# Merge stage of a decoder trunk: raw tiles of their own for the second attention's results, and two blocks' gates loaded ahead of them

## The chip, the cores and the metric

The kernel runs on one core of one Trainium2 chip. The time is the device time of that core in microseconds, from the first instruction to the last; the kernel before takes 1337.81 us (median of 3 runs, 1337.39 to 1337.92). Engines are named as in the profile: PE multiplies matrices (PEld is its weight load), DVE and POOL are the two elementwise engines, ACT evaluates functions and copies, SP issues DMAs in the order in which they stand in its queue. Each engine executes its own list in order; engines wait for each other through semaphores.

## What is computed

One layer of a decoder trunk on 1024 tokens of width 1024: a norm, two attentions side by side, a gated merge of their results, a residual, and a gated MLP with a short convolution. The part that matters here is the merge:

```python
def reference(x, ...):
    xn = rmsnorm(x, norm_mix_w[l])
    proj = xn @ w_in[l]
    da_q, da_k, da_v, sw_q, sw_k, sw_v, g_da, g_sw = split_cols(proj)
    ...
    y_da = diff_attention(da_q, da_k, da_v, lam, lam_init, subln_w[l])
    y_sw = sliding_window_attention(sw_q, sw_k, sw_v, sinks[l])
    merged = jax.nn.sigmoid(g_da) * (y_da @ w_br_da[l]) + jax.nn.sigmoid(g_sw) * (y_sw @ w_br_sw[l])
    x = x + merged @ w_mix_out[l]
    ...
```

Both results `y_da` and `y_sw` are 1024 tokens by 512 channels; everything is float32.

## The kernel before

Tensors lie transposed, channels on the 128 partitions and the 1024 tokens (T) along the row; a tile of [P, T] is 128 x 1024 floats, 512 KB. A product in float32 is made of three products of rounded parts: an operand is split into a high part (`h`, a cast on ACT) and a low part (`l`, the difference, on DVE), and PE adds `wh*xh`, `wh*xl` and `wl*xh` (lines 212 to 214). Half of T, 512 columns, is one matmul.

The two attentions write their results to `yd` in DRAM, 8 tiles: 0 to 3 from the differential attention, 4 to 7 from the sliding-window attention (the second attention), whose last piece is stored by ACT's queue at the very end of that stage. The gates' raw products lie in `gd`, 16 tiles.

`rest` is the stage after the attentions, the merge. It has three steps.

1. Loop over c = 0..7: load `yd[c]` into a raw tile `yr`, and split it into `yh[c]` (ACT, line 836) and `yl[c]` (DVE, line 837). The raw tiles come from a pool `yrp` of 4, so that tile 4 takes the place of tile 0 when that has been split, and so on. Between them the last four half blocks of the gates' projection are computed on PE (`back_half`, matmuls `g<-xh,wh`, lines 212 to 214).
2. For each output block m = 0..7, `first(m)`: take the block's weights (`next_w`: load, `wh` on ACT line 177, `wl` on DVE line 179); load the block's two gates `gr` (line 796), multiply them by the norm factor on POOL (line 797), take the sigmoid on ACT (line 804); multiply the first attention's four tiles with the weights into the PSUM tile `sc`; and multiply gate 0 by `sc` on DVE (line 808). For m = 0 the products with `yl` stand last (line 203).
3. `second(m)`: the same product for the second attention's four tiles, in two halves of T into PSUM tiles `g` from a pool of 2; DVE multiplies gate 1 by each half (line 816), adds the two branches (line 821), and the sum is split again (lines 822, 823).

The order is `first(0), first(1), second(0), second(1)`, then `first(m), second(m)` for m = 2..7. The gates have 4 tiles in all, so the first two blocks' gates fill them. A scheduler orders each engine's list from the program's order and priorities; `tc.high_priority(200)` in step 1 lets the loads of `yd` go ahead of what is written before them. A DMA in SP's queue that has to wait for a tile holds all that stand behind it. After step 3, `mix` multiplies the merged tiles with the next weights.

## Time and profile before

| what | value |
|---|---|
| median of 3 runs | 1337.81 us |
| the profiled execution: its own time | 1339.47 us |
| the profiled execution: its span, first to last instruction | 1337.7 us |
| mean granted TensorE clock | 0.997 |
| last store of the second attention's results issued | 499.86 us |
| merge stage, first high part of `yd` to first matmul of the mix | 502.1 to 606.5 us |
| loads of the second four `yd` tiles: issue to landing, shortest, median, longest | 3.2, 5.8, 7.5 us |
| all 16 gate loads: issue to landing, shortest, median, longest | 3.1, 4.0, 8.7 us |

The times of the rows are counted from the span's start. In a view of the timeline a row is: start, duration, engine, line, operation, result<-operands, shapes, how many in a row, and in brackets the idle time of the engine before it with what ended it. Ends of matmuls are modelled: a matmul of 512 columns is shown with 0.39 us, while the next starts 0.227 us after it.

### The profile page before, as it was taken

How to read it: one execution, taken by the hardware profiler on the slowest of the kernel's cores; microseconds unless marked ns; L12 is line 12 of the kernel's file. 1: busy time of each engine (PE TensorE's matmuls, PEld its weight loads, DVE VectorE, ACT ScalarE, POOL GpSimd, SP SyncE). 2: the span in 40 equal slices, each digit the busy share in tenths (PEclk: the TensorE clock that was granted, in tenths of full speed). 3: DMA queues.
4: the chain of work that ended last, by engine and by line, in shares of the span. 5: the costliest groups of instructions: out<-in, count | busy, mean ns of one | idle time of the engine just before them, and what ended most of it. 6: DMA issues, size and time to landing. Idle time of an engine off the chain costs nothing.

```text
span 1337.7 us, 17292 instructions
## 1 busy us (share of the span) xinstructions
PE 1319.4 (99%) x6264; PEld 1096.8 (82%) x6264; DVE 1075.5 (80%) x1607; ACT 624.4 (47%) x1023; POOL 483.1 (36%) x363
## 2 busy tenths in 40 slices
PE   7999999999999999999999999999999999999997
PEld 6888888888888777888888888888888888888887
DVE  8847775289889877765678999999999997879975
ACT  8432232176667766433445443344444444323553
POOL 0336543000102113521436556555565520214532
PEclk9999999999999999999999999999999999999998
DMA  7423443866553335434432222222222229672263
GB/s 259 145 107 142 158 158 142 251 179 174 157 128 125 104 112 212 149 117 132 136 111 84 90 93 82 80 78 95 79 96 75 75 84 332 214 279 67 95 173 126
DMA packets 63621, 183.69 MB, mean 137 GB/s; under 512 B 6960, under 2 KB 15280, under 8 KB 63536
## 3 DMA queue, kind: packets, MB, share of 16 engines
q1 hardware_dynamic: 51504, 164.13, 37.5%
q10 hardware_dynamic: 11456, 17.41, 3.6%
q0 software_dynamic: 576, 1.05, 0.5%
q8 instruction: 49, 0.80, 0.3%
q14 instruction: 36, 0.29, 0.1%
HBM read 130.66 MB, written 50.86 MB: 136 GB/s over the span
## 4 chain that ended last, share of the span: by engine, by line
PE 93%; DVE 3%; POOL 1%; issue 1%; DMA 1%; ACT 1%; POOLq 0%; SPq 0%; ACTq 0%; DVEq 0%
PE t L924 13%; PE t L923 13%; PE t L925 13%; PE g L212 4%; PE g L213 4%; PE g L214 4%; PE sc L213 3%; PE sc L214 3%; PE sc L212 3%; PE t L917 3%; PE sc L639 3%; PE y L1167 2%; PE d L1167 2%; PE d L924 2%; PE d L923 2%; PE d L925 2%
## 5 line engine op out<-in xcount | busy, mean ns | idle before, releaser
L1097 ACT ACTIVATE c<-us,vecs 128x512 f32<-128x512 f32 x80 | 61.3, 781 | 134.0 <-POOL us L1091 130.0
L1099 DVE SCALAR_TENSOR_TENSOR c<-us,vecs,c 128x512 f32<-128x512 f32 x160 | 110.5, 748 | 8.6 <-ACT c L1097 8.6
L1091 POOL TENSOR_TENSOR us<-us,rstd 128x1024 f32<-128x1024 f32 x38 | 99.7, 2643 | 4.5 <-DVE us L472 2.4
L129 DVE TENSOR_TENSOR sl<-sf,sh 128x1024 fp32r<-128x1024 f32 x62 | 86.6, 1399 | 11.5 <-ACT sh L128 11.5
L128 ACT CAST sh<-sf 128x1024 fp32r<-128x1024 f32 x62 | 63.4, 1049 | 59.8 <-PE t L924 43.5
L129 DVE TENSOR_TENSOR wl<-raw,wh 128x1024 fp32r<-128x1024 f32 (+1 forms) x35 | 76.6, 2190 | 3.7 <-ACT wh L128 3.6
L177 ACT CAST wh<-raw 128x1024 fp32r<-128x1024 f32 (+2 forms) x46 | 46.2, 1005 | 67.8 <-PE sc L213 30.4
L104 POOL TENSOR_TENSOR sf<-rv 128x512 f32<-128x512 f32 x30 | 41.3, 1377 | 100.7 <-DVE sl L129 57.8
L212 PE MATMUL g<-xh,wh 128*128 128x512 f32 x176 | 70.7, 402 | 0.1
L214 PE MATMUL g<-xh,wl 128*128 128x512 f32 x176 | 70.4, 400 | 0.0
L213 PE MATMUL g<-xl,wh 128*128 128x512 f32 x176 | 70.2, 399 | 0.0
L179 DVE TENSOR_TENSOR wl<-raw,wh 128x1024 fp32r<-128x1024 f32 (+2 forms) x46 | 53.8, 1169 | 17.5 <-PE t L609 11.0
L109 POOL TENSOR_TENSOR sf<-raw,rv 128x512 f32<-128x512 f32 x30 | 40.8, 1359 | 66.0 <-DVE sl L129 66.0
L643 DVE CUSTOM_DVE_ANT_0 L<-sc,bias 128x128 f32<-128x128 f32 (+7 forms) x64 | 47.8, 752 | 17.0 <-PE sc L639 13.9
L622 POOL MEMSET aT<- 128x128 f32 x32 | 6.2, 205 | 151.6 <-PE t L668 97.9
L797 POOL TENSOR_TENSOR gr<-gr,rstd 128x1024 f32<-128x1024 f32 x16 | 41.0, 2566 | 52.9 <-DMA gr<-gd 43.5
L644 ACT ACTIVATE L<-L,sm 128x128 f32<-128x128 f32 (+7 forms) x64 | 49.6, 779 | 20.0 <-DVE sm L643 13.5
L129 DVE TENSOR_TENSOR wl<-rv,wh 128x512 fp32r<-128x512 f32 x30 | 49.8, 1661 | 3.5 <-ACT wh L128 3.5
L1101 ACT ACTIVATE c<-c 128x512 f32<-128x512 f32 x40 | 24.0, 600 | 60.7 <-DVE c L1099 60.7
L639 PE MATMUL sc<-u,u 128*128 128x512 f32 (+2 forms) x192 | 49.7, 358 | 0.0
L878 POOL TENSOR_TENSOR rstd<-rstd,t 128x512 f32<-128x512 f32 x14 | 21.7, 1558 | 76.1 <-ACT t L877 76.1
L212 PE MATMUL sc<-mh,wh 128*128 128x512 f32 x126 | 49.0, 389 | 0.0
(529 smaller groups left out, 4423.6 us busy)
## 6 DMA issues: line engine op xcount, KB each, us to landing
u<-qd SPq DMA_DIRECT2D x72, 256.0 KB, 6.2
raw<-in_w_in SPq DMA_DIRECT2D x25, 512.0 KB, 4.1
raw<-in_w_up SPq DMA_DIRECT2D x23, 512.0 KB, 3.5
hr<-hd SPq DMA_DIRECT2D x46, 256.0 KB, 5.7
hd<-c SPq DMA_DIRECT2D x22, 512.0 KB, 2.6
rv<-in_w_up SPq DMA_DIRECT2D x21, 512.0 KB, 3.5
raw<-in_w_down SPq DMA_DIRECT2D x19, 512.0 KB, 4.1
gr<-gd SPq DMA_DIRECT2D x16, 512.0 KB, 4.0
```

The source lines that it names most:

```text
L128: i = nc.scalar.copy(hi, src)
L129: j = nc.vector.tensor_tensor(lo, src, hi.bitcast(F32), ALU.subtract)
L212: nc.tensor.matmul(ps, wh[:, kc + o, :], ah, start=first and n == 0, stop=False)
L213: nc.tensor.matmul(ps, wh[:, kc + o, :], al, start=False, stop=False)
L214: nc.tensor.matmul(ps, wl[:, kc + o, :], ah, start=False, stop=last and n == len(kcs) - 1)
L639: nc.tensor.matmul(sc[:, lo + n0:lo + n1], qs, k[c][part][:, n0:n1], start=part == 0, stop=part == 1)
L923: nc.tensor.matmul(ps, ah[:, k, :], bh, start=first and n == 0, stop=False, skip_group_check=skip)
L924: nc.tensor.matmul(ps, ah[:, k, :], bl, start=False, stop=False, skip_group_check=skip)
L925: i = nc.tensor.matmul(ps, al[:, k, :], bh, start=False, stop=last and n == len(ks) - 1, skip_group_check=skip)
L1091: (nc.vector if j == 0 else nc.gpsimd).tensor_tensor(u[:, 2:], u[:, 2:], self.rstd, ALU.mult)
L1097: nc.scalar.activation(c, u[:, o + 2:o + 2 + H2], AF.Identity, bias=self.vecs[:, C_CB + m:C_CB + m + 1], scale=col(m, 2))
L1099: nc.vector.scalar_tensor_tensor(c, u[:, o + k:o + k + H2], col(m, k), c, ALU.mult, ALU.add)
```

## The change

The second attention's four raw tiles get a pool of their own, `ysp`, so that they no longer wait for the first four to be split. Ahead of them, at priority 300, the four gates of the first two blocks are loaded; `first` takes these and loads the gates itself only for the later blocks.

```diff
                 bp = bctx.enter_context(tc.tile_pool(name="bp", bufs=2, reuse_waits="tile"))
+                ysp = bctx.enter_context(tc.tile_pool(name="ysp", bufs=4, reuse_waits="tile"))
                 parts = []
+                gates = {}
                 for c in range(8):
+                    if c == 4:
+                        with tc.high_priority(300):
+                            for m in range(2):
+                                gates[m] = [self.tl(bp, [P, T], "gr", bufs=4) for _ in range(2)]
+                                for br, g in enumerate(gates[m]):
+                                    nc.sync.dma_start(g, self.gd[8 * br + m])
                     with tc.high_priority(200):
-                        r = self.tl(yrp, [P, T], "yr")
+                        r = self.tl(ysp if c > 3 else yrp, [P, T], "yr")
                         nc.sync.dma_start(r, self.yd[c])
...
                     for br in range(2):
-                        g = self.tl(bp, [P, T], "gr", bufs=4)
-                        nc.sync.dma_start(g, self.gd[8 * br + m])
+                        if m in gates:
+                            g = gates[m][br]
+                        else:
+                            g = self.tl(bp, [P, T], "gr", bufs=4)
+                            nc.sync.dma_start(g, self.gd[8 * br + m])
                         i = nc.gpsimd.tensor_tensor(g, g, self.rstd, ALU.mult)
```

No instruction is added or left out; the lists have the same length. From line 779 on the new file's line numbers are higher (783 becomes 791, 797 becomes 808, 804 becomes 815, 808 becomes 819, 816 becomes 827, 836 and 837 become 847 and 848).

SP's queue at the turn from attention to merge, before. The names are those of the tiles above; `gr_5078` and `gr_5082` are block 0's gates, `gr_5118` and `gr_5122` block 1's; the semaphores DMAHW tell of the landing of earlier DMAs, which share eight of them.

```order
L796 DMA gr_5078<-gd 128x1024 [waits DMAHW1_49,PE_49,Pool_49]
L796 DMA gr_5082<-gd 128x1024 [waits DMAHW2_49,PE_49,Pool_49]
L783 DMA yr_5044<-yd 128x1024 [waits DMAHW6_49,DMAHW5_49,DMAHW7_49,DMAHW3_49,DVE_49]
L783 DMA yr_5050<-yd 128x1024 [waits DMAHW4_49,DVE_49]
L783 DMA yr_5056<-yd 128x1024 [waits DMAHW7_49,DMAHW5_49,DVE_49]
L783 DMA yr_5062<-yd 128x1024 [waits DVE_49]
L796 DMA gr_5118<-gd 128x1024 [waits DMAHW0_49,Pool_49]
L796 DMA gr_5122<-gd 128x1024 [waits DMAHW1_49]
```

The same place of SP's queue in the changed kernel (block 0's gates are `gr_5047` and `gr_5048`, block 1's `gr_5051` and `gr_5052`):

```order
L788 DMA gr_5047<-gd 128x1024 [waits DMAHW1_49,PE_49,Pool_49]
L788 DMA gr_5048<-gd 128x1024 [waits DMAHW2_49,PE_49,Pool_49]
L788 DMA gr_5051<-gd 128x1024 [waits DMAHW3_49,Pool_49]
L788 DMA gr_5052<-gd 128x1024 [waits DMAHW4_49]
L791 DMA yr_5055<-yd 128x1024 [waits DMAHW6_49,DMAHW7_49,DMAHW5_49,Pool_49]
L791 DMA yr_5061<-yd 128x1024 [waits DMAHW7_49]
L791 DMA yr_5067<-yd 128x1024 [waits DMAHW0_49]
L791 DMA yr_5073<-yd 128x1024 [waits DMAHW1_49]
```

Block 1's two gates have moved ahead of the four loads of `yd`, and these no longer wait for DVE. The waits for Pool in both are for POOL's work in the attention stage.

DVE's list at the start of the merge, before:

```order
L837 TENSOR_TENSOR yl_4933<-yr_4930,yh_4932 128x1024
L837 TENSOR_TENSOR yl_4967<-yr_4964,yh_4966 128x1024
L837 TENSOR_TENSOR yl_5007<-yr_5004,yh_5006 128x1024
L837 TENSOR_TENSOR yl_5041<-yr_5038,yh_5040 128x1024
L179 TENSOR_TENSOR wl_5076<-raw_5072,wh_5074 128x1024
L837 TENSOR_TENSOR yl_5047<-yr_5044,yh_5046 128x1024
L837 TENSOR_TENSOR yl_5053<-yr_5050,yh_5052 128x1024
L837 TENSOR_TENSOR yl_5059<-yr_5056,yh_5058 128x1024
L837 TENSOR_TENSOR yl_5065<-yr_5062,yh_5064 128x1024
L808 TENSOR_TENSOR gr_5078<-gr_5078,sc_5086 128x1024
L808 TENSOR_TENSOR gr_5118<-gr_5118,sc_5126 128x1024
L816 TENSOR_TENSOR gr_5082<-gr_5082,g_5152 128x512
```

and in the changed kernel:

```order
L848 TENSOR_TENSOR yl_4936<-yr_4933,yh_4935 128x1024
L848 TENSOR_TENSOR yl_4970<-yr_4967,yh_4969 128x1024
L848 TENSOR_TENSOR yl_5010<-yr_5007,yh_5009 128x1024
L848 TENSOR_TENSOR yl_5044<-yr_5041,yh_5043 128x1024
L179 TENSOR_TENSOR wl_5087<-raw_5083,wh_5085 128x1024
L819 TENSOR_TENSOR gr_5047<-gr_5047,sc_5093 128x1024
L848 TENSOR_TENSOR yl_5058<-yr_5055,yh_5057 128x1024
L848 TENSOR_TENSOR yl_5064<-yr_5061,yh_5063 128x1024
L848 TENSOR_TENSOR yl_5070<-yr_5067,yh_5069 128x1024
L819 TENSOR_TENSOR gr_5051<-gr_5051,sc_5129 128x1024
L848 TENSOR_TENSOR yl_5076<-yr_5073,yh_5075 128x1024
L827 TENSOR_TENSOR gr_5048<-gr_5048,g_5155 128x512
```

The two products of a gate with `sc` have moved in between the second attention's low parts: block 0's ahead of all four, block 1's ahead of the last. On ACT the sigmoids of block 0's second gate and of block 1's first gate have moved ahead of the casts `yh` of the second attention's tiles. PE's list differs in one place: in `second(0)` the last two matmuls of the first half (those with the last `yl` and with `wl`) have moved behind the first two of the second half. POOL's list is the same: the first two blocks' four gates, one after the other, then the later blocks' gates.

## The prediction

> **What bounds the kernel now.** First the page's busy shares and its chain by engine: PE works 99% of the span and holds 93% of the chain. What the change is worth is therefore the time that PE stands still at the start of the merge, and no more.

> ```profile
> PE 1319.4 (99%) x6264; PEld 1096.8 (82%) x6264; DVE 1075.5 (80%) x1607; ACT 624.4 (47%) x1023; POOL 483.1 (36%) x363
> PE 93%; DVE 3%; POOL 1%; issue 1%; DMA 1%; ACT 1%; POOLq 0%; SPq 0%; ACTq 0%; DVEq 0%
> ```

> Then the busy time by stretch (a row begins with the stretch, its length and PE's busy time; clock, DMA share and GB/s end it): PE is idle between 517.2 and 525.1 alone, and not at all in the rest of the merge.

> ```profile
> 500.00:517.20 17.20, 17.20 (x77) 14.24 (x76) 11.55 (x8) 11.43 (x12) 4.79 (x2) 1.00 0.70 264
> 517.20:525.10 7.90, 6.02 (x26) 4.33 (x25) 4.30 (x5) 4.79 (x5) 5.64 (x2) 1.00 0.50 202
> 525.10:606.00 80.90, 80.90 (x357) 67.00 (x358) 55.17 (x47) 29.04 (x29) 30.55 (x12) 1.00 0.38 130
> ```

> PE's timeline shows the two places.

> ```profile
> 519.30 0.39 PE L212 MATMUL g<-yh,wh 128*128 128x512 f32 x1
> 519.83 0.50 PE L213 MATMUL g<-yl,wh 128*128 128x512 f32 x1
> 520.17 0.40 PE L214 MATMUL g<-yh,wl 128*128 128x512 f32 x1
> 522.91 0.39 PE L214 MATMUL g<-yh,wl 128*128 128x512 f32 x1
> 525.03 0.50 PE L212 MATMUL g<-yh,wh 128*128 128x512 f32 x1 [1.73 <-DVE gr L816]
> 525.37 0.40 PE L213 MATMUL g<-yl,wh 128*128 128x512 f32 x1
> ```

> Matmuls otherwise start 0.227 us apart (511.82 to 512.27 below is two steps). From 519.30 to 519.83 is 0.53, so 0.30 is lost, and 0.11 more, since the one after a wait follows after 0.34. From 522.91 to 525.03 is 2.12: 1.89 lost, and again 0.11. Together 0.41 + 2.00 = 2.41 us. The chain of waits says what the longer one hangs on:

> ```profile
> 509.99 0.32 SPq L783
> 510.41 8.26 DMA gr<-gd
> 518.74 3.30 POOL gr L797
> 522.06 1.07 ACT gr L804
> 523.16 1.22 DVE gr L808
> 524.38 0.61 DVE gr L816
> ```

> Block 1's first gate is issued behind the last load of `yd`, lands 8.26 us later, and goes through POOL, ACT and DVE; only then comes line 816, which frees the PSUM tile that PE needs for `second(1)`.

> **What is taken away.** Block 1's gates are issued right behind block 0's, whose loads were issued by 494.98 + 3.57 = 498.55 and landed 4.0 and 5.6 us after their issue; over all gate loads the longest took 8.7.

> ```profile
> 494.98 3.57 SPq L796 DMA_DIRECT2D gr<-gd  x2
> DMA to landing us min/median/max: 4.0/4.8/5.6
> DMA to landing us min/median/max: 3.1/4.0/8.7
> ```

> So they land between 502.6 and about 508 instead of 518.7, and line 816 of block 0 needs no gate of block 1 any more. The second attention's loads then wait only for stores, the last issued at 499.86:

> ```profile
> 499.86 0.39 ACTq L560 DMA_DIRECT2D yd<-ys  x1
> DMA to landing us min/median/max: 1.8/3.2/8.7
> DMA to landing us min/median/max: 3.2/5.8/7.5
> ```

> With the longest landing of a store (8.7, second row) and of these loads (7.5, third row) they are there by 516.1, which is early enough for all that follows. Their cost is nothing: SP has no other work there. Gain if nothing else moved: 2.41 us.

> **What is added.** No instruction. But POOL's multiplies of block 1's gates move too: from 518.7, where DVE was mostly reading PSUM, to right behind block 0's, that is onto DVE's run of low parts.

> ```profile
> 500.69 4.79 POOL L797 TENSOR_TENSOR gr<-gr,rstd 128x1024 f32<-128x1024 f32 x2 [7.44 <-DMA gr<-gd]
> 503.23 6.74 DVE L837 TENSOR_TENSOR yl<-yr,yh 128x1024 fp32r<-128x1024 f32 x4 [3.56 <-ACT yh L836]
> 506.48 3.49 DVE L837 TENSOR_TENSOR yl<-yr,yh 128x1024 fp32r<-128x1024 f32 x3
> 509.89 1.21 DVE L179 TENSOR_TENSOR wl<-raw,wh 128x1024 fp32r<-128x1024 f32 x1
> 510.01 1.98 PE L203 MATMUL sc<-yl,wh 128*128 128x512 f32 x8
> 511.82 0.39 PE L212 MATMUL sc<-yh,wh 128*128 128x512 f32 x1
> 512.27 0.39 PE L214 MATMUL sc<-yh,wl 128*128 128x512 f32 x1
> ```

> The first low part starts at 503.23 and does not end before POOL does (500.69 + 4.79 = 505.48); three more follow 1.14 us apart ((3.49 - 1.21)/2), the fourth ends at 509.97, block 1's `wl` at 511.10. PE's eight products with `yl` come at 510.01, each pair just in time, and the first with `wl` at 512.27. The cover is thin: 1.17 us for `wl`, 1.4 for the last `yl` (509.97 against the last pair, at 510.01 + 6 x 0.227 = 511.37).

> [...]

> ```profile
> 698.19 2.27 POOL L109 TENSOR_TENSOR sf<-raw,rv 128x512 f32<-128x512 f32 x1
> 700.43 2.27 POOL L108 TENSOR_TENSOR sf<-sf,raw 128x512 f32<-128x512 f32 x1
> 702.77 1.30 POOL L110 TENSOR_TENSOR sf<-raw,sf 128x512 f32<-128x512 f32 x1
> 695.89 1.22 DVE L837 TENSOR_TENSOR T_2l<-t,T_2h 128x1024 fp32r<-128x1024 f32 x1
> 697.02 2.29 DVE L837 TENSOR_TENSOR T_3l<-xw,T_3h 128x1024 fp32r<-128x1024 f32 x1
> 699.24 2.31 DVE L129 TENSOR_TENSOR wl<-raw,wh 128x1024 fp32r<-128x1024 f32 x1
> ```

> They take turns, one instruction each: DVE's ends at 699.31 and 701.55 are 2.24 apart instead of 1.14, POOL's rows last 2.27 where one alone lasts 1.30. A POOL instruction let in between thus delays DVE by 1.10, its own 1.30 less 0.20. A gate multiply alone lasts 2.42:

> ```profile
> L797 POOL TENSOR_TENSOR gr<-gr,rstd x16: 2388/2418/3292, 500.7 to 584.7; 128x1024 f32<-128x1024 f32 x16
> ```

> so each costs 2.22. The third and fourth gates have landed while DVE is still in its run (505.48 to 511.10), so I let both in: 4.44 us. The fourth `yl` ends at 514.41, `wl` at 515.54. PE does the last pair with `yl` at 514.46 (0.05 for the semaphore), starts `first(1)` at about 515.0 and its first product with `wl` at 515.59 instead of 512.27: 3.32 later, with 0.11 for the restart 3.4. Whether POOL's two go in ahead of the second and third `yl` or later does not matter: the end of `wl` counts both. Bounds: none let in, 0; one, 2.22 less, which is 1.2; both, 3.4.

> The moved line 808 on DVE (819 now) takes one operand from PSUM and is not delayed: at 523.16 above it lasted 1.22 while POOL was at work (518.74 and 5.64 us on, by the second row of the stretches). That of block 1 stands ahead of the last `yl` and waits for the end of `first(1)`: `second(0)` starts at 517.26 + 3.4 = 520.7 (517.26 is 511.82 and 24 steps), line 819 runs 1.2 us from about 520.9, the last `yl` ends at 523.3, and PE, whose list has two other matmuls ahead of it now, needs it at 520.7 + 11 x 0.227 = 523.2. About 0.2 with the restart. Line 816 then frees its PSUM tile at about 524.8, well ahead of `second(1)` at 526.3: the longer stall is gone.

> **The sum.** 3.4 - 2.41 + 0.2 = +1.2 us. After 525 every wait is counted from PE's, DVE's or POOL's own progress and PE has no idle time to fill or to save, so the shift stays to the end. The profiled execution takes 1339.47 (its span 1337.7), 1.7 over the median of the runs shown; the same shift gives 1340.7 there, and on the median 1337.81 a forecast of **1339.0**. With small waits more or less, the forecast's own range is 1338.0 to 1339.8.

> **Rivals.** [...] *Only one gets in* because the fourth gate lands after DVE's run is over: 1.2 - 2.22 = -1.0, so 1336.8; the landing would have to be later than the longest of the 16.

> *The clock drops.* My sum makes PE wait from about 511.1 to 513.3 for the third `yl` (the turns end it at 513.27), and some 0.4 us more for the fourth. In the tail the granted clock (third number from the end) is 1.00, then 0.50, after a stretch with nothing but 12 narrow matmuls:

> ```profile
> 1327.70:1329.70 2.00, 1.47 (x12) 1.30 (x11) 0.77 (x4) 1.58 (x4) 0.08 (x1) 1.00 0.84 296
> 1329.80:1337.70 7.90, 1.12 (x4) 0.72 (x4) 1.88 (x3) 0.37 (x1) 1.78 (x2) 0.50 0.44 152
> ```

> That is 2 us of little work; the wait of 1.73 us above left it at 1.00. So the point from which this decides lies near 2 us in one piece. At half clock a matmul takes 0.454. No row shows how long it lasts in work: between nothing and the 7.9 us of the tail, a loss of 0 to 4.0; halfway, 2.0: 1339.0 + 2.0 = 1341.0, slower. Against it: PE is busy before, between and after the two waits, and the tail is one case. [...]

> **Chances.** Forecast 0.62; port no matter 0.13; one gets in 0.10; clock drops 0.15. Range for 8 in 10: from the first rival, 1335.4, to 1340.5, which leaves out most of the clock's case. A measurement of this kernel tells a change from none at about 0.2%, 2.7 us. Faster by that (under 1335.1) would need more than all the idle time of the stage: 0.04. Slower by that (over 1340.5) is the clock's case, most of it: 0.13. Within: 0.83.

> **What would show it.** POOL's four multiplies in a row from 500.7 with the later ones lasting 3.3 instead of 2.4; low parts of 3.3 us on DVE; `wl` ending at 515.5; a wait of about 2.2 us on PE among the products of line 203, released by DVE's `yl`; no wait at `second(1)`; the first matmul of the mix some 1.2 us later. Wrong if the four low parts end by 510 with POOL busy beside them, if block 1's gates land after 510, or if the clock's row in 510 to 520 is under 1.00.

## The result, and the profile after

| | before | after |
|---|---|---|
| median of 11 runs each | 1337.81 us | 1340.88 us |
| lowest and highest run | 1336.05, 1339.88 | 1338.69, 1342.42 |
| profiled execution: own time, span | 1339.47, 1337.7 | 1341.0, 1339.2 |

The ratio is 1.0021, with a 95% interval of 1.0012 to 1.0029: 1.6 to 3.9 us slower. The forecast was 1339.0 and the range ended at 1340.5. The direction was right, the size was not: the time is that of a rival, *the clock drops*, at 1341.0.

First the two engines that were to take turns, POOL and then DVE, on the timeline of the kernel after (start, duration, engine, line, what, how many; in brackets the idle time ahead and what ended it):

```profile
500.53 11.46 POOL L808 TENSOR_TENSOR gr<-gr,rstd 128x1024 f32<-128x1024 f32 x4 [7.60 <-DMA gr<-gd]
```

```profile
502.91 11.30 DVE L848 TENSOR_TENSOR yl<-yr,yh 128x1024 fp32r<-128x1024 f32 x4 [3.57 <-ACT yh L847]
514.14 1.21 DVE L179 TENSOR_TENSOR wl<-raw,wh 128x1024 fp32r<-128x1024 f32 x1
```

POOL's four multiplies run in a row, and the four low parts take 11.30 us instead of 6.74. The single instructions end in turn: DVE's first at 506.39, POOL's third at 508.67, DVE's second at 509.75, POOL's fourth at 511.99, DVE's third at 513.08. Block 1's `wl` ends at 515.35 (515.5 forecast). PE's timeline shows what that does to block 0's products with `yl` (line 203), and one thing more:

```profile
509.69 1.07 PE L203 MATMUL sc<-yl,wh 128*128 128x512 f32 x4
513.13 0.73 PE L203 MATMUL sc<-yl,wh 128*128 128x512 f32 x2 [2.37 <-DVE yl L848]
514.27 1.22 PE L203 MATMUL sc<-yl,wh 128*128 128x512 f32 x2 [0.40 <-DVE yl L848]
515.28 0.63 PE L212 MATMUL sc<-yh,wh 128*128 128x512 f32 x1
515.71 0.63 PE L213 MATMUL sc<-yl,wh 128*128 128x512 f32 x1
516.14 0.63 PE L214 MATMUL sc<-yh,wl 128*128 128x512 f32 x1
516.56 0.63 PE L212 MATMUL sc<-yh,wh 128*128 128x512 f32 x1
516.99 0.49 PE L213 MATMUL sc<-yl,wh 128*128 128x512 f32 x1
517.32 0.39 PE L214 MATMUL sc<-yh,wl 128*128 128x512 f32 x1
```

The wait of 2.37 us, ended by DVE's third `yl`, is the one forecast at about 2.2. Behind it the matmuls start 0.427 apart (515.28, 515.71, 516.14) instead of 0.227. The view by stretch gives the clock granted there; a row is the stretch, its length, the busy time of PE, PEld, DVE, ACT and POOL, and then the granted clock, the DMA share and GB/s:

```profile
506.95:510.36 3.41, 3.41 (x16) 2.81 (x15) 3.41 (x2) 3.38 (x5) 3.41 (x2) 1.00 0.63 200
510.36:513.77 3.41, 1.04 (x4) 0.30 (x2) 3.41 (x2) 3.41 (x5) 1.63 (x1) 1.00 0.89 363
513.77:517.19 3.42, 3.02 (x8) 2.37 (x8) 3.17 (x4) 1.84 (x2) 0.00 (x0) 0.50 0.16 44
517.19:520.60 3.41, 3.41 (x17) 2.78 (x16) 3.03 (x3) 0.00 (x0) 0.00 (x0) 1.00 0.76 233
...
521.60:529.50 7.90, 7.90 (x36) 6.45 (x36) 5.19 (x6) 2.22 (x3) 0.00 (x0) 1.00 0.23 66
```

For 3.41 us the clock is at half, right behind a stretch of the same length in which PE was busy for 1.04 us only. The last row holds `second(0)`, which starts at 521.66, and the start of `second(1)` at 527.12, the two places at which the kernel before lost its 2.41 us: PE is busy for all of it, so both old waits are gone.

The first matmul of the mix shows the sum, before and then after:

```profile
595.88 0.39 PE L212 MATMUL sc<-mh,wh 128*128 128x512 f32 x1
```

```profile
597.84 0.39 PE L212 MATMUL sc<-mh,wh 128*128 128x512 f32 x1
```

Below, *the stage* is the time from the first product with `yh` (506.38 before, 506.06 after) to this matmul: 89.50 us before, 91.77 after. (The 606.5 us in the table ahead of the prediction is the time of a later matmul of the mix; the first stands at 595.88.) It is freer of chance than the whole time, which also holds what differs between runs ahead of the stage and in the tail.

### The profile page after: what moved, and what is told of

Its sections match the earlier page's. It is cut to its first block, busy times and chain, and to the rows that moved or that the text cites. A ratio compares the mean times of both kernels' runs of the same rounds, so it can differ in the third digit from the quotient of the medians.

```text
span 1339.2 us, 17291 instructions
## 1 busy us (share of the span) xinstructions
PE 1320.1 (99%) x6264; PEld 1097.4 (82%) x6264; DVE 1082.9 (81%) x1607; ACT 623.5 (47%) x1023; POOL 484.0 (36%) x363
## 4 chain that ended last, share of the span: by engine, by line
PE 94%; DVE 3%; POOL 1%; issue 1%; ACT 1%; DMA 0%; POOLq 0%; SPq 0%; ACTq 0%; DVEq 0%
PE t L936 13%; PE t L935 13%; PE t L934 13%; PE g L212 4%; PE g L213 4%; PE g L214 4%; PE sc L212 3%; PE sc L213 3%; PE sc L214 3%; PE t L928 3%; PE sc L639 3%; PE y L1178 2%; PE d L1178 2%; PE d L935 2%; PE d L934 2%; PE d L936 2%
## 5 line engine op out<-in xcount | busy, mean ns | idle before, releaser
L129 DVE TENSOR_TENSOR sl<-sf,sh 128x1024 fp32r<-128x1024 f32 x62 | 87.4, 1412 | 11.5 <-ACT sh L128 11.5
L129 DVE TENSOR_TENSOR wl<-raw,wh 128x1024 fp32r<-128x1024 f32 (+1 forms) x35 | 76.7, 2191 | 3.7 <-ACT wh L128 3.6
L212 PE MATMUL g<-xh,wh 128*128 128x512 f32 x176 | 70.6, 401 | 0.1
L214 PE MATMUL g<-xh,wl 128*128 128x512 f32 x176 | 70.4, 400 | 0.0
L213 PE MATMUL g<-xl,wh 128*128 128x512 f32 x176 | 70.3, 399 | 0.0
L179 DVE TENSOR_TENSOR wl<-raw,wh 128x1024 fp32r<-128x1024 f32 (+2 forms) x46 | 53.8, 1169 | 18.3 <-PE t L609 11.0
L109 POOL TENSOR_TENSOR sf<-raw,rv 128x512 f32<-128x512 f32 x30 | 40.7, 1356 | 65.6 <-DVE sl L129 65.6
L808 POOL TENSOR_TENSOR gr<-gr,rstd 128x1024 f32<-128x1024 f32 x16 | 41.4, 2596 | 54.6 <-DMA gr<-gd 45.3
L129 DVE TENSOR_TENSOR wl<-rv,wh 128x512 fp32r<-128x512 f32 x30 | 49.3, 1642 | 3.5 <-ACT wh L128 3.5
L212 PE MATMUL sc<-mh,wh 128*128 128x512 f32 x126 | 49.0, 389 | 0.0
```

The lines of the kernel that those rows point to most:

```text
L129: j = nc.vector.tensor_tensor(lo, src, hi.bitcast(F32), ALU.subtract)
L212: nc.tensor.matmul(ps, wh[:, kc + o, :], ah, start=first and n == 0, stop=False)
L213: nc.tensor.matmul(ps, wh[:, kc + o, :], al, start=False, stop=False)
L214: nc.tensor.matmul(ps, wl[:, kc + o, :], ah, start=False, stop=last and n == len(kcs) - 1)
```

## The experiments

In the kernels' expectations, "the whole change" is the kernel after. Table of all profiled executions, each time from the trace: the stage; from the first product with `yh` to the start of `second(0)`, and from there to `second(1)`; whether a stretch of half clock stands in the merge; the median time (number of runs); and the ratio to the kernel before on the same chip.

| kernel | stage | to `second(0)` | to `second(1)` | half clock | median us | ratio, 95% interval |
|---|---|---|---|---|---|---|
| before | 89.50 | 10.88 | 7.77 | no | 1337.81 (11) | |
| b1, before again | 89.07 | 10.88 | 7.31 | no | 1338.47 (1) | |
| b2, before again | 88.62 | 10.88 | 6.88 | no | 1337.44 (1) | |
| after | 91.77 | 15.60 | 5.46 | yes | 1340.88 (11) | 1.0021 [1.0012, 1.0029] |
| a1, after again | 91.28 | 15.10 | 5.46 | yes | 1341.15 (1) | |
| a2, after, a third time | 92.17 | 16.01 | 5.44 | yes | 1340.62 (12) | 1.0022 [1.0013, 1.0031] |
| e1, tiles only | 88.03 | (other order) | | no | 1337.41 (11) | 0.9996 [0.9987, 1.0004] |
| e2, gates only | 91.57 | 15.36 | 5.49 | yes | 1341.12 (11) | 1.0021 [1.0012, 1.0030] |
| e3, multiplies held | 88.34 | 10.88 | 6.74 | no | 1337.90 (11) | 1.0000 [0.9991, 1.0008] |
| e5, held, and ACT's order | 88.19 | 10.88 | 6.59 | no | 1337.52 (11) | 0.9999 [0.9990, 1.0008] |
| e4, wait filled, 9 | 90.07 | 13.91 | 5.44 | no | 1340.31 (11) | 1.0015 [1.0006, 1.0023] |
| e6, wait filled, 9 on two tiles | 89.95 | 13.79 | 5.44 | no | 1340.60 (11) | 1.0019 [1.0010, 1.0027] |
| e7, wait filled, 4 | 89.98 | 13.82 | 5.44 | no | 1340.80 (12) | 1.0022 [1.0013, 1.0030] |
| e8, wait filled, 2 | 90.01 | 13.85 | 5.44 | no | 1341.19 (8) | 1.0025 [1.0014, 1.0036] |

Medians of the kernel before, run beside them, were 1337.91 (e1 to e4), 1337.49 (b1, b2, a1, e5), 1337.82 (a2, e6, e7) and 1337.91 (e8).

### e1: the tiles alone

```diff
-                    if c == 4:
+                    if False:
```

> The second four results keep tiles of their own (ysp); the gates of blocks 0 and 1 are loaded where the kernel before loaded them, so that those of block 1 are issued behind the last yr load. Theory (DVE and POOL take turns; the wait that this makes on PE halves the clock for one 3.41 us stretch): block 1's gates land after the first four yl are done, POOL has only block 0's two multiplies beside them, and block 0's low products start as before: no wait of 2.4 us before them, no 0.50 clock row in the merge. From the first yh product to the first mix matmul 87.1 to 89.5 us (before 89.50, whole change 91.77), the time 1335.4 to 1338 us. Rival (the new tiles are what delays the merge, through the loads' order): a wait of 2 us or more stays before the products of L203 and the stage takes 91 us or more, as in the whole change.

```profile
511.18 11.11 POOL L808 TENSOR_TENSOR gr<-gr,rstd 128x1024 f32<-128x1024 f32 x4 [18.55 <-DMA gr<-gd]
```

```profile
502.59 9.17 DVE L848 TENSOR_TENSOR yl<-yr,yh 128x1024 fp32r<-128x1024 f32 x8 [3.56 <-ACT yh L847]
```

With POOL's multiplies behind them, all eight low parts take 9.17 us, 1.15 each; there is no wait at line 203 and no half clock. The stage is 88.03. The rival falls: the new tiles delay nothing. The schedule is another one, though: all of `yd` is split early, block 1's weights come later, and `second(0)` now runs ahead of `first(1)`. So e1 clears the tiles, but does not price POOL's multiplies beside DVE's low parts.

### e2: the gates ahead alone

```diff
-                        r = self.tl(ysp if c > 3 else yrp, [P, T], "yr")
+                        r = self.tl(yrp, [P, T], "yr")
```

> The gates of blocks 0 and 1 are loaded ahead; all eight results share the four yrp tiles as before. Theory: POOL's four multiplies run in a row beside the first four yl as in the whole change, so yl are 3.4 us each, block 0's low products wait over 2 us and the clock is 0.50 for one stretch; the second four yr, which wait for those yl, land later than before (517.44 for the last), so that second(0) waits too. Stage 91.8 to 94 us against 89.50 before, time 1340 to 1342.5 us. Rival (the delay belongs to the new tiles): stage 89.5 or less, time 1338 or less.

It is the whole change over again: 91.57 (a little under the 91.8 to 94 expected), with the half clock, and 1341.12 us. The wait for the third `yl` is 1.89 us, not over 2, and one part of what was expected did not come: `second(0)` does not wait for the later loads, 5.49 us to `second(1)`. So both the loss and the removal of the old waits belong to the gates, and the tiles add nothing to either.

### e3: the same loads, POOL's multiplies held

```diff
+        self.low_of = {**getattr(self, "low_of", {}), id(wl): self.lo}; return wh, wl
...
-                        if m == 0:
+                        if m < 2:
-                            tc.add_manual_dep(i.ins, self.last.ins.name,
+                            tc.add_manual_dep(i.ins, (self.low_of[id(w[1])] if m else self.last).ins.name,
```

> The whole change, with one order added: POOL's two multiplies of block 1's gates start only when DVE has written block 1's wl, so they no longer stand beside the first four yl. The loads, the tiles and every engine's order are those of the whole change. Theory (turns of DVE and POOL): two of the first four yl go back to 1.2 us, wl ends near 511 instead of 515.35, the wait of 2.4 us before the products of L203 is gone, no 0.50 clock row in the merge; the third sigmoid, which stands ahead of yh4 to yh7 on ACT, comes at 513 instead of 510.8, which second(0) hardly feels. Stage 87.1 to 88.0 us against 89.50 before and 91.77 in the whole change; time 1335.4 to 1336.5 us. Rival (the four loads ahead, or the order of the loads, make the delay): the wait stays and the time is 1340 to 1341.

```profile
499.50 4.78 POOL L808 TENSOR_TENSOR gr<-gr,rstd 128x1024 f32<-128x1024 f32 x2 [6.93 <-DMA gr<-gd]
509.98 4.79 POOL L808 TENSOR_TENSOR gr<-gr,rstd 128x1024 f32<-128x1024 f32 x2 [5.70 <-DVE wl L179]
```

```profile
502.56 6.21 DVE L848 TENSOR_TENSOR yl<-yr,yh 128x1024 fp32r<-128x1024 f32 x4 [3.56 <-ACT yh L847]
508.69 1.21 DVE L179 TENSOR_TENSOR wl<-raw,wh 128x1024 fp32r<-128x1024 f32 x1
```

Loads, tiles and the order on every engine are those of the change; only two POOL instructions wait 5.70 us for block 1's `wl`. The low parts take 6.21 us instead of 11.30, `wl` ends at 509.90 instead of 515.35, `second(0)` starts at 10.88 again, and the clock stays. This is the cleanest proof of the first term: not the transfers, but POOL's two multiplies beside DVE's run made the wait. The size was missed: the stage is 88.34 instead of 87.1 to 88.0, the time 1337.90, the same as before, instead of 1335.4 to 1336.5. A wait of 0.84 us is left in `second(0)`:

```profile
518.04 1.21 DVE L819 TENSOR_TENSOR gr<-gr,sc 128x1024 f32<-128x1024 f32 x1
```

```profile
520.44 0.50 PE L213 MATMUL g<-yl,wh 128*128 128x512 f32 x1 [0.84 <-DVE yl L848]
```

DVE does block 1's product (line 819) ahead of the last `yl`, and PE waits for that.

### b1, b2, a1: both kernels profiled again

> The kernel before, unchanged, profiled once more: its first profile's own time (1339.47) is 1.6 us above the median of its runs. If the waits of 0.41 and 2.00 us that the sum took as won belong to every run, the stage from the first yh product to the first mix matmul is 89.5 us again; if they belong to that one run, it is 88 us or less and the sum gave the change up to 2 us too much.

> As the run ahead: 89.5 us for the stage if the two waits are in every run, between 87.1 and 89 if they come and go with the transfers' landing; the place to look at is the last yr load, which landed 7.45 us after its issue in the first profile.

> The whole change, profiled once more. Theory: the wait before the products of L203 comes from the order on POOL and DVE, so it is 2.4 us again; the stretch of half clock is 3.41 us long again and begins where PE has been mostly idle for 3.41 us before it; its place moves with the phase of the windows, so the stage is 91.8 us with the stretch and 90.4 without it (2 of 11 runs were about 2 us shorter than the others).

The wait at `second(1)` of the kernel before, in b1 and then in b2, each with the gate's transfer on which the chain of waits shows it to hang:

```profile
524.11 0.50 PE L212 MATMUL g<-yh,wh 128*128 128x512 f32 x1 [1.68 <-DVE gr L816]
```

```profile
509.49 8.11 DMA gr<-gd
```

```profile
523.33 0.50 PE L212 MATMUL g<-yh,wh 128*128 128x512 f32 x1 [1.28 <-DVE gr L816]
```

```profile
508.92 7.88 DMA gr<-gd
```

The mechanism of the first profile is there each time, its size is not: 1.73 us, 1.68, 1.28. The gate's transfer starts 4.03 us after the first product with `yh` in the first profile (510.41 - 506.38), 3.57 in b1 and 3.36 in b2, and takes 8.26, 8.11 and 7.88 us; the smaller wait of 0.41 is only in the first. What the change can win here is 7.77, 7.31 or 6.88 less 5.46: 2.31, 1.85, 1.42, in the mean 1.9 and not 2.41.

a1 repeats the change: half clock for 3.41 us from 514.79, stage 91.28. The wait was expected at 2.4 us again and is not. The first row is a1, the second the change a third time (a2, below):

```profile
512.80 0.73 PE L203 MATMUL sc<-yl,wh 128*128 128x512 f32 x2 [1.56 <-DVE yl L848]
```

```profile
513.90 0.74 PE L203 MATMUL sc<-yl,wh 128*128 128x512 f32 x2 [2.57 <-DVE yl L848]
```

In a1 it is 1.56 us and stands before the third pair, in a2 2.57 us before the fourth. POOL's multiplies and DVE's low parts meet a little differently each time: block 1's `wl` ends 9.28 us after the first product with `yh` in the first profile of the change, 8.47 in a1 and 9.21 in a2.

### e5: e3 with the sigmoids of block 1 behind `yh` 4 to 7

```diff
-                        with tc.issue_after(self.hi.ins) if br else nullcontext():
+                        with tc.issue_after((y7 if m == 1 else self.hi).ins) if br or m == 1 else nullcontext():
```

(`y7` is ACT's copy of the last `yh`.)

> e3 with the sigmoids of block 1's gates behind yh4 to yh7 on ACT; in the schedule yl7 then also stands ahead of block 1's product on DVE. Everything else as in e3 (stage 88.34, one wait of 0.84 us at 519.6, which ends with yl7). Theory: no wait over 0.25 us is left on PE, the stage is 87.3 to 87.7 us, 1.8 to 2.2 under the first profile of before; the time 1336 to 1337.3 us, faster than both kernels by 0.05 to 0.15%. Rival (the sigmoid of block 1's first gate, now later, holds DVE's product and with it a PSUM tile): a wait of 0.5 us or more before second(1), stage 88.3 or more, time as e3's 1337.9.

```profile
519.73 0.50 PE L213 MATMUL g<-yl,wh 128*128 128x512 f32 x1 [0.16 <-DVE yl L848]
520.87 0.51 PE L213 MATMUL g<-yl,wh 128*128 128x512 f32 x1 [0.17 <-DVE yl L848]
```

The 0.84 has become several waits of under 0.2 us for the low parts, with 1.1 us lost in all (6.59 to `second(1)` instead of 5.45); the stage is 88.19, not 87.3 to 87.7, and the time 1337.52 against 1337.49. Neither e1, e3 nor e5 beats the kernel before by what can be measured. The profiles say that 0.7 to 1.0 us of the stage is won (88.0 to 88.3 against the mean of 89.06 of the three profiles of before), at most 0.08%, no more than the half width of the intervals.

### e4, e6, e7, e8: PE's wait filled, and a2 beside them

Matmuls on operands that are there, into spare PSUM tiles that nothing reads, stand between the second and the third pair of line 203, so that the delay by `yl` stays and PE is idle for less of it.

```diff
+        (wh, wl), idle = w, [self.tl(self.psT, [P, H2], "t") for _ in range(2 if fill else 0)]
...
         for n, kc in enumerate(kcs):
+            [nc.tensor.matmul(idle[k % 2], wh[:, kc + o, :], act(kc, 0)[0], start=k < 2, stop=k >= fill - 2) for k in range(fill if n == 2 else 0)]
             for ps, hf in zip(pss, halves):
                 nc.tensor.matmul(ps, wh[:, kc + o, :], act(kc, hf)[1], start=False, stop=n == len(kcs) - 1)
```

(`fill` is 9 in e6, 4 in e7, 2 in e8, for block 0 alone; e4 has 9 in one tile. In e7 the four take 1.07 us, 0.227 from start to start; by that nine are, as an estimate, 2.0 us of work inside the wait of 2.4 us.)

> [...] Theory (the wait costs twice, once itself and once by the clock): yl late as in the whole change, third pair at the same time, but no 0.50 clock row in the merge: stage 91.77 - 1.3 = 90.5 us, time 1339.0 to 1339.6 us. Rival 1 (the clock row has nothing to do with PE's idleness): the row of 3413 ns stays, stage 91.8, time 1340.9. Rival 2 (the nine matmuls themselves push the third pair back): stage 92 or more.

> The whole change, unchanged, timed and profiled beside the two kernels with fill on the same chip. Theory: own time 1340.9 in the median as before, one stretch of 0.50 clock of 3413 ns in the merge, stage 91.3 to 91.8 us.

> e4 with its nine matmuls spread over two spare PSUM tiles (five and four), so that the tiles of the later stages fall on the same banks as in the whole change (in e4 they had moved by one, and a wait of 0.33 us at 1178 stood there that no other run has). Theory (the half clock costs 1.2 to 1.7 us): stage 90.0 to 90.6, no 0.50 row in the merge, median 1.2 to 1.7 under that of the whole change in this call. Rival (the clock is free, or PE's extra work costs what the clock saves): within 0.5 of the whole change.

> As e6 with four matmuls in place of nine: 0.9 us of work, so that some 1.1 to 1.5 us of the wait before the third pair is left, and 0.4 before the fourth. In the three profiles of kernels with the half clock PE was idle for 2.0 to 2.7 us of the 3.41 us ahead of it; in the one with nine matmuls for 0.4; in the kernel before a wait of 2.0 us that lay across two windows (1.2 and 0.8) left the clock at 1.00. If idleness of under half a window is let pass, no 0.50 row here, stage 90.0 to 90.6, median as e6; if the third of a window that is idle here is enough, the row of 3413 ns is there and the time is that of the whole change.

> As e7 with two matmuls in place of four, to see from which idleness the clock falls. So far PE was busy for 1.04, 1.57 and 1.58 us (by the profile's modelled ends) of the 3.41 us ahead of the three stretches of half clock, and for 2.39, 2.51 and 2.59 us of a window with a wait in it behind which the clock stayed at 1.00. Two matmuls add 0.45 us: 1.5 to 2.0 us busy, depending on the phase. If the limit is at half a window (1.7) or above, the 0.50 row is there and the stage is 91.3 to 92.2 us; if it lies just above 1.58, there is none and the stage is 90.0 us.

PE in e7, where a wait of 0.82 us is left ahead of the third pair:

```profile
510.83 1.07 PE L201 MATMUL t<-yh,wh 128*128 128x512 f32 x4
512.72 0.73 PE L203 MATMUL sc<-yl,wh 128*128 128x512 f32 x2 [0.82 <-DVE yl L848]
513.86 0.74 PE L203 MATMUL sc<-yl,wh 128*128 128x512 f32 x2 [0.40 <-DVE yl L848]
514.44 0.40 PE L212 MATMUL sc<-yh,wh 128*128 128x512 f32 x1
```

The low parts come late as in the change, but behind the wait there is no half clock (granted 1.00 from 513.65 to 517.06). What the half clock costs is estimated from the start of `second(0)`, here in e7 with the `wl` on which it hangs, and in the change (its `wl` is shown above):

```profile
513.72 1.21 DVE L179 TENSOR_TENSOR wl<-raw,wh 128x1024 fp32r<-128x1024 f32 x1
520.12 0.39 PE L212 MATMUL g<-yh,wh 128*128 128x512 f32 x1
```

```profile
521.66 0.39 PE L212 MATMUL g<-yh,wh 128*128 128x512 f32 x1
```

In e7, `second(0)` starts 5.18 us after the end of `wl`, and in the other fills 5.17 to 5.19. In the three profiles of the change it starts 6.32, 6.63 and 6.79 us after it. If PE at the clock of 1.00 had waited for `wl` there too, as in the fills, the half clock costs 1.14 us in the first profile, 1.45 in a1 and 1.61 in a2, in the mean 1.40. From the step of the matmuls the estimate for a stretch that is all work is 1.60: 3.41 us with matmuls 0.427 apart instead of 0.227 lose 3.41 x (1 - 0.227/0.427). The rest is the delay: the end of `wl`, 9.28, 8.47 or 9.21 us after the first product, plus 5.18, less the 10.88 of the kernel before, is 3.58, 2.77 or 3.51, in the mean 3.29. (In the fills `wl` ends 8.60 to 8.73 us after the first product, so their delay is 2.9 to 3.0.)

What PE did ahead of a half clock is read by cutting the trace at the edges of the half-clock stretches. The two drops in the trace of the kernel after, at 513.77 and in the tail at 1332.97, are 240.0 x 3.413 us apart. Where the merge has no half clock, the cuts (the windows of the expectations) are therefore counted back from the drop in the tail in steps of 3.413 us; that something is decided at those points too is an assumption, since the clock does not change there. The change a third time (a2), then e8, e7 and the kernel before, each with the cut that holds the wait, and, but for e7, the one behind:

```profile
512.06:515.47 3.41, 1.57 (x6) 1.06 (x7) 3.41 (x3) 3.31 (x4) 0.70 (x1) 1.00 0.27 108
515.47:518.89 3.42, 3.42 (x10) 2.64 (x9) 3.42 (x4) 0.00 (x0) 0.00 (x0) 0.50 0.66 178
```

```profile
509.42:512.83 3.41, 2.10 (x9) 1.16 (x7) 3.41 (x2) 3.41 (x5) 1.62 (x1) 1.00 1.01 410
512.83:516.24 3.41, 3.01 (x13) 2.17 (x13) 3.41 (x4) 2.44 (x3) 0.00 (x0) 1.00 0.33 55
```

```profile
510.24:513.65 3.41, 2.39 (x10) 1.34 (x8) 3.41 (x2) 3.21 (x4) 1.34 (x1) 1.00 0.96 351
```

```profile
520.79:524.20 3.41, 2.51 (x12) 1.72 (x10) 1.16 (x2) 2.09 (x2) 3.41 (x2) 1.00 0.11 46
524.20:527.62 3.42, 2.59 (x11) 2.17 (x12) 3.39 (x5) 1.81 (x2) 0.18 (x1) 1.00 0.00 0
```

PE busy for 1.04 us of the cut (after), 1.13 (e2), 1.57 (a2) or 1.58 (a1): half clock in the next. Busy for 2.10 (e8), 2.39 (e7), 2.51 or 2.59 (before): none. No row here lies between 1.58 and 2.10. The kernel before has a wait of 1.73 us too (523.30 to 525.03); the counted edge at 524.20 cuts it into 0.90 and 0.83, and the clock stays at 1.00. That it stays because of the edge is not shown.

In the tail of the same trace, that of the kernel before, the busy time alone does not tell the cuts apart:

```profile
1326.34:1329.75 3.41, 2.83 (x24) 2.64 (x22) 2.13 (x5) 1.58 (x4) 0.96 (x2) 1.00 0.73 256
1329.75:1333.16 3.41, 1.12 (x4) 0.72 (x4) 1.88 (x3) 0.37 (x1) 1.75 (x2) 0.50 0.28 99
```

Here PE is busy for 2.83 us of a cut, and the next is at half clock all the same. Twelve of the 24 matmuls have a single column (128x1); without them PE is busy for 1.36. In the traces of the two kernels, from the start of the clock's record to the drop in the tail, the three cuts ahead of a drop hold 0.72 and 1.04 us (after) and 1.36 (before) when counted so, and no other holds less than 1.87.

The whole times do not follow. With the half clock gone and a delay of 2.96 left, the medians of the fills should be near 1339 us (2.96 - 1.9 = 1.1 over the kernel before); they are 1340.31, 1340.60, 1340.80 and 1341.19, under the change's (1340.88, 1340.62) by 0.6 at most or not at all, with intervals of about 1.2 us each way. By the medians, e6's rival (within 0.5 of the whole change) holds.

Each run lists its mean clock. Of the change's 24 runs 16 had 0.996 and 3 had 0.998; of the 22 runs with nine matmuls none had 0.996 and 16 had 0.998, so the half clock is gone there in most (a mean of 0.998 is, by 0.002 x 1338 / 0.5, about 5 us of half clock, and the tail alone takes 6.2 us within the span in the trace of the kernel after and 7.9 in that of before). With four or two it is not gone in all: two of 12 and two of 8 runs at 0.996. The change's own runs speak for the clock: the three at 0.998 took 1338.69, 1338.72 and 1339.07, the 16 at 0.996 1340.94 in the median. But they are three runs without a trace, and a shorter wait would spare both itself and the drop. The 16 runs with nine matmuls at 0.998 took 1340.35 in the median.

Part of what is missing is seen: in e4 and e6 a new wait of 0.33 us stands at 1178, in a later stage (spreading the nine over two tiles did not remove it, and with four or two there is none). The rest stays open. The profiled executions of the fills (1340.12, 1339.49, 1339.54, 1338.92) are faster than their medians, and only of these is there a trace.

## Why the prediction was wrong

By its own steps:

- **POOL's two multiplies go onto DVE's run, one instruction each in turn: +3.4.** Right in mechanism and in size. POOL's four in a row, three low parts of 3.4 us and `wl` at 515.35 were all as forecast. e3 takes the two away from there and the wait goes; the three profiles of the change put the term at 3.58, 2.77 and 3.51, mean 3.29. POOL's two multiplies did not stay out of DVE's run (the case of 1335.4, the lower end of the range, *port no matter* among the chances), and not only one of them got in: both fall with the first two rows above.
- **The waits removed: -2.41.** Both are gone (last row of the stretches, and 5.46 us to `second(1)` in the table), but the size was read from one execution, whose own time is 1.7 over the median. In three profiles it is 2.31, 1.85 and 1.42, mean 1.9. The sum was moved to the median as it stood, although a term that hangs on the landing of a transfer was part of what made that execution long.
- **Line 819 ahead of the last `yl`: +0.2.** Nothing was lost there: 5.46 us from `second(0)` to `second(1)`, which is 24 steps of 0.227. In e3 the same order leaves a wait of 0.84, since there `second(0)` comes early.
- **The clock, left out of the sum: 0.** This is the step that failed. The prediction set the deciding point "near 2 us in one piece", had PE waiting for 2.2 and then 0.4 us at 1.00 all the same, and gave the drop 0.15. It had the granted clock of the tail to say that 2 us of little work may be enough, and argued against it that PE was busy before, between and after. In the merge the profiles have the clock at 0.50 behind the cuts of 3.41 us in which PE was busy for 1.04 to 1.58 us, and at 1.00 behind those above with 2.10 to 2.59; in the kernel after, the wait of 2.37 us (510.76 to 513.13) lies in one such cut as a whole. Its own test, a clock row under 1.00 between 510 and 520, came out against it: 0.50 from 513.77 to 517.19. By the estimate above it cost 1.40 us in the mean of the three profiles, against the 2.0 taken as halfway between 0 and 4.0. A matmul took 0.427 there; the 0.454 was an estimate, twice 0.227, that no run shows.

3.29 - 1.9 + 0 + 1.40 = +2.8 us; the stage gives 91.74 - 89.06 = +2.7 (means of three profiles each), the medians +3.07 and, in the second comparison, 1340.62 - 1337.82 = +2.80. The sum of 1.2 lacked 1.40 for the clock and gave the removed waits 0.5 too much; in the other direction the first term and line 819 were 0.1 and 0.2 too high. With the clock's term alone put right, the forecast is 1340.4. That the clock's term is real in the stage is shown by the traces, by taking idleness away and leaving the delay; that the whole time is shorter by as much without it is not shown, and the medians of the fills speak against it.

## What to carry to other kernels

## What the runs showed of the hardware that was not expected

With the loads ahead, a small store lands later. The last store of the second attention's results (128 KB) lands 8.2 us after its issue in the kernel after, 4.5 in e1, where the gates go later, and 3.5 in the kernel before. The rows are those of the DMA issues from 497 to 510, after, e1 and before:

```profile
yd<-ys ACTq DMA_DIRECT2D x1, 128.0 KB, 8.2
```

```profile
yd<-ys ACTq DMA_DIRECT2D x1, 128.0 KB, 4.5
```

```profile
yd<-ys ACTq DMA_DIRECT2D x1, 128.0 KB, 3.5
```

It is 7.2 to 8.3 us in all ten profiles with the two blocks' gates ahead, and 2.7 to 3.5 in the three of the kernel before. In e2 it is 7.2 although no load of these results is issued before 506.26, so the gates alone are enough. In the kernel after, that store lands at 507.72, and the second of the four loads of its results is issued at 507.74. The first had landed at 507.55; the other three landed at 511.48 to 514.00 (before: 509.83, then 513.43 to 517.44). PE did not wait for them here.
